# RMSNorm and swish over 16,384 rows: row groups of 32, 36, 28 and 32, rows 48 to 79 loaded in two transfers, rows 32 to 95 stored as 18, 18 and 28

## The chip, the cores and the metric

The kernel runs on one core of one Trainium2 chip. The metric is the device time of one execution in microseconds (us). Before the change the median of three runs is 159.67 us, with the lowest at 159.59 and the highest at 159.82. A difference of under 0.2%, which is 0.32 us here, counts as no change.

## The reference

The input x has 16 x 1024 rows of 512 float32 numbers. Every row is divided by its root mean square, multiplied by gamma, and passed through swish:

```python
rms = np.sqrt(np.mean(x ** 2, axis=-1, keepdims=True) + eps)
x_norm = x / rms * gamma
return (x_norm * (1.0 / (1.0 + np.exp(-x_norm)))).astype(np.float32)
```

So 33.55 MB go in, 33.55 MB come out, and every row is worked on by itself.

## The kernel before

The 16,384 rows are dealt to 128 partitions, so that each partition has 128 rows of 2 KB. From here on "row" means a row of one partition (0 to 127), which stands for 128 rows of x, or 256 KB. The rows are cut into four **groups** (line 28: 32, 48, 16 and 32 rows). A group is a contiguous stretch of x and of the output. Inside it, partition p owns a contiguous run of as many rows as the group has (function `dram`, lines 100 to 106). The group's size is therefore the distance in memory from one partition's piece to the next: 64, 96, 32 and 64 KB. A transfer moves a run of rows for all 128 partitions, and it must lie within one group.

In on-chip memory the rows lie in a **ring** of 96 (line 29). Row a sits at place a modulo 96, and the result is written over the input. Rows 0 to 95 have places of their own. Rows 96 to 127 take the places of rows 0 to 31, so they may be loaded only when the store of rows 0 to 31 has finished.

**Transfers.** All of them are issued by SyncE (SP), in the order of the list `order` (lines 33 to 37), and they all go through one queue. The list holds "load" and "store" entries, "landed" (SP waits until a load has arrived, line 166) and "stored" (SP waits until store 0 has finished, line 169). A store waits itself until enough units have gone through swish (`need` at lines 120 to 123, with the count in `ends`, line 56). Before the change the order is: loads 0, 4, 8, gamma, loads 16, 24, 32, 48, 64, 75; wait until load 64 has landed; store 0 (32 rows, needs four units); load 80; wait until store 0 has finished; loads 96, 112, 125; wait until load 112 has landed; stores 32, 64, 80, 96, 120. A load or store is named here by its first row.

**Compute.** It goes in 16 **units** of 8 rows (`cn`, line 39), numbered from 0. For each unit ScalarE (ACT) squares and sums six of the rows (line 215), VectorE (DVE) the other two (line 251). GpSimd (POOL) makes the factor 1/rms of it (lines 183 and 189). DVE multiplies the unit's rows by the factor and gamma (line 260), and ACT applies swish in one instruction of 4096 elements for each partition (line 225; line 245 for the last two units). ACT's loop squares unit k and then applies swish to unit k - 2. TensorE computes nothing: it passes on that a unit's loads have arrived (lines 172 to 176), so that ACT may start with its squares. Unit k waits for every load that begins in its eight rows.

Of the kernel before, what the change touches and what calls it, by code (L numbers as in the profile page):

```python
# [9 lines left out]
def kernel(  # L10
# [14 lines left out]
    of = out.flatten_outer_dims()  # L25
    R, D = xf.shape

    groups = [32, 48, 16, 32]
    ring = 96
    loads = [(0, 4), (4, 4), (8, 8), (16, 8), (24, 8), (32, 16), (48, 16), (64, 11), (75, 5)]  # L30
    loads += [(80, 16), (96, 16), (112, 13), (125, 3)]
    stores = [(0, 32), (32, 32), (64, 16), (80, 16), (96, 24), (120, 8)]
    order = [("load", a) for a in (0, 4, 8)] + [("gamma", 0)]
    order += [("load", a) for a in (16, 24, 32, 48, 64, 75)]
    order += [("landed", 64), ("store", 0), ("load", 80)]
    order += [("stored", 0), ("load", 96), ("load", 112), ("load", 125)]
    order += [("landed", 112)] + [("store", a) for a in (32, 64, 80, 96, 120)]
    early = 2
    cn = 8
    own = 2  # L40
# [285 lines left out]
```

## Time and profile before

| What | us |
|---|---|
| median of three runs | 159.67 |
| the profiled execution's own time | 159.75 |
| its span, first to last instruction | 158.4 |
| ACT busy | 115.7 (73%) |
| DVE busy | 107.7 (68%) |
| POOL busy | 42.9 (27%) |
| time of the transfers' packets, share of 16 DMA engines' span | 99.1% |

The span begins with the first load's issue. 67.12 MB were moved at a mean of 424 GB/s over it. In the rows for transfers, the time "to landing" counts from the start of the issue on SP to the arrival of the last part. Because the queue works off its transfers one after another, the difference between the landings of two neighbours is the time that the later one took to be moved.

### The profile page before, as it was taken

To read this page: it belongs to the slowest core of one execution; us is meant where nothing else is said; L and a number is where in the kernel's file an instruction comes from. 1 tells how busy PE (TensorE), PEld (TensorE's weight loads), DVE (VectorE), ACT (ScalarE), POOL (GpSimd) and SP (SyncE) were. 2 spreads that over 40 slices of the span, in tenths; PEclk is the share of its full clock that TensorE was granted. 3 is DMA by queue.
4 is the path that set the end of the run, shared out by engine and by line. 5 is a ranking of instruction groups with operands and counts; after the bars stand their busy time and mean duration, and the time that the engine had idled before them with its cause. 6 is when DMAs were issued, how large, how long until landed. Compare 5 with 4: busy or idle time off the path is not lost. (4 is left out here: it accounts for less than half of the span.)

```text
span 158.4 us, 844 instructions
## 1 busy us (share of the span) xinstructions
DVE 107.7 (68%) x198; ACT 115.7 (73%) x205; POOL 42.9 (27%) x38
## 2 busy tenths in 40 slices
DVE  0051899798989889898925989989898995000000
ACT  3608389999999999999459999999999385400000
POOL 1031426060524426060601433516061500000000
DMA  7999999999999979799999999996969999999997
GB/s 257 451 416 443 422 488 439 397 406 497 389 395 565 463 331 530 314 381 480 406 406 472 399 430 400 550 513 281 530 298 488 406 397 455 538 397 397 397 397 331
DMA packets 2744, 67.12 MB, mean 424 GB/s; under 512 B 308, under 2 KB 308, under 8 KB 440
## 3 DMA queue, kind: packets, MB, share of 16 engines
q1 hardware_dynamic: 2744, 67.12, 99.1%
HBM read 33.56 MB, written 33.55 MB: 424 GB/s over the span
## 5 line engine op out<-in xcount | busy, mean ns | idle before, releaser
L260 DVE SCALAR_TENSOR_TENSOR xb<-xb,rstd,gamma_sb 128x512 f32 (+1 forms) x128 | 86.1, 745 | 0.0
L215 ACT ACTIVATE junk<-xb 128x512 f32 (+1 forms) x94 | 54.6, 581 | 13.1 <-ACTq L98 11.3
L225 ACT ACTIVATE xb<-xb x14 | 50.5, 3604 | 0.7 <-ACTq L98 0.7
L251 DVE SCALAR_TENSOR_TENSOR junk_v<-xb 128x512 f32 (+1 forms) x34 | 22.1, 689 | 23.0 <-DVEq L98 23.0
L189 POOL TENSOR_TENSOR rstd<-aeps,neg_half 128x8 f32<-128x8 f32 x16 | 31.7, 1984 | 1.3
L183 POOL TENSOR_SCALAR aeps<-ms 128x8 f32<-128x8 f32 x16 | 10.4, 648 | 79.1 <-DVE junk_v L251 79.1
L215 ACT ACTIVATION_READ_ACCUMULATOR junk<-xb 128x1 f32 x94 | 17.7, 188 | 0.0
L245 ACT ACTIVATE xb<-xb 128x4096 f32<-128x4096 f32 x2 | 7.2, 3616 | 5.0 <-DVE xb L260 5.0
L251 DVE DVE_READ_ACCUMULATOR junk_v<-xb 128x1 f32 x34 | 2.8, 82 | 0.0
L227 ACT ACT_TABLE_LOAD x1 | 1.3, 1283 | 1.9 <-PEq L62 1.9
L269 DVE LOAD_MASK_SELECT gamma_sb<-gamma x1 | 0.0, 14 | 2.0 <-DMA gamma<-in_gamma_dram 2.0
L178 POOL MEMSET gamma<- 128x512 f32 x1 | 0.5, 524 | 1.5 <-POOLq L62 1.5
L269 DVE STREAM_SHUFFLE gamma_sb<-gamma 128x512 f32<-128x512 f32 x1 | 0.7, 719 | 0.0
L307 POOL MEMSET const-float32-0.0<- 128x1 f32 x1 | 0.1, 98 | 0.2 <-issue 0.2
L179 POOL MEMSET neg_half<- 128x8 f32 x1 | 0.1, 104 | 0.0
L307 POOL MEMSET const-bfloat16-1.0<- 128x1 bf16 x1 | 0.1, 103 | 0.0
L307 POOL MEMSET const-uint8-127<- 128x1 uint8 x1 | 0.1, 102 | 0.0
L307 POOL MEMSET const-float32-1.0<- 128x1 f32 x1 | 0.1, 99 | 0.0
## 6 DMA issues: line engine op xcount, KB each, us to landing
xb<-in_x_dram SPq DMA_DIRECT2D x4, 4096.0 KB, 29.9
out_dram<-xb SPq DMA_DIRECT2D x2, 4096.0 KB, 29.8
xb<-in_x_dram SPq DMA_DIRECT2D x3, 2048.0 KB, 14.1
out_dram<-xb SPq DMA_DIRECT2D x1, 6144.0 KB, 22.4
xb<-in_x_dram SPq DMA_DIRECT2D x1, 3328.0 KB, 27.0
xb<-in_x_dram SPq DMA_DIRECT2D x1, 2816.0 KB, 43.1
xb<-in_x_dram SPq DMA_DIRECT2D x2, 1024.0 KB, 6.0
out_dram<-xb SPq DMA_DIRECT2D x1, 2048.0 KB, 21.9
```

Of the source, the lines that this page charges most:

```text
L178: nc.gpsimd.memset(gamma4, 0.0).then_inc(s_zero, 1)
L179: nc.gpsimd.memset(neg_half, -0.5).then_inc(s_half, 1)
L183: nc.gpsimd.tensor_scalar(out=aeps[k % 2], in0=ms[min(k, 1)], scalar1=eps_f, scalar2=None, op0=ALU.add,),
L189: nc.gpsimd.tensor_tensor(out=rstd[:, k * cn : (k + 1) * cn], in0=aeps[k % 2], in1=neg_half, op=ALU.pow),
L215: nc.scalar.activation(out=dummies[j], in_=rows[j], func=AF.Square, scale=inv_d**0.5, accum_out=sums[:, j : j + 1],)
L225: nc.scalar.activation(out=rows, in_=rows, func=AF.Silu).then_inc(s_swish, 1)
L227: nc.scalar.preload_act_table_set("silu_and_others")
L245: nc.scalar.activation(out=rows, in_=rows, func=AF.Silu), s_norm, n + 1
L251: ins = nc.vector.scalar_tensor_tensor(out=junk_v[j], in0=rows[j], scalar=inv_d, in1=rows[j], op0=ALU.mult, op1=ALU.mult, accum_out=to[:, ...
L260: ins = nc.vector.scalar_tensor_tensor(out=rows[j], in0=rows[j], scalar=factors[j], in1=gamma_sb, op0=ALU.mult, op1=ALU.mult,)
L269: need(nc.vector.stream_shuffle(gamma_sb, gamma4, [0] * 32), s_gld, 16).then_inc(s_gamma, 1)
L307: nc = _bacc.Bacc("TRN2", target_bir_lowering=False, num_devices=1)
```

## The change

Three lists and one wait change; no instruction on the compute engines does.

- The groups are 32, 36, 28 and 32 rows for 32, 48, 16 and 32. The distances between the partitions' pieces in the two middle groups become 72 and 56 KB.
- Rows 48 to 79 are loaded as 20 and 12 rows (loads 48 and 68) for 16, 11 and 5 (loads 48, 64 and 75). There is one load fewer.
- Rows 32 to 95 are stored as 18, 18 and 28 rows (stores 32, 50 and 68) for 32, 16 and 16 (stores 32, 64 and 80). The number of stores stays the same.
- Ahead of store 0 SP waits for the landing of load 48, not of load 64.

```diff
-    groups = [32, 48, 16, 32]
+    groups = [32, 36, 28, 32]
     ring = 96
-    loads = [(0, 4), (4, 4), (8, 8), (16, 8), (24, 8), (32, 16), (48, 16), (64, 11), (75, 5)]
+    loads = [(0, 4), (4, 4), (8, 8), (16, 8), (24, 8), (32, 16), (48, 20), (68, 12)]
     loads += [(80, 16), (96, 16), (112, 13), (125, 3)]
-    stores = [(0, 32), (32, 32), (64, 16), (80, 16), (96, 24), (120, 8)]
+    stores = [(0, 32), (32, 18), (50, 18), (68, 28), (96, 24), (120, 8)]
     order = [("load", a) for a in (0, 4, 8)] + [("gamma", 0)]
-    order += [("load", a) for a in (16, 24, 32, 48, 64, 75)]
-    order += [("landed", 64), ("store", 0), ("load", 80)]
+    order += [("load", a) for a in (16, 24, 32, 48, 68)]
+    order += [("landed", 48), ("store", 0), ("load", 80)]
     order += [("stored", 0), ("load", 96), ("load", 112), ("load", 125)]
-    order += [("landed", 112)] + [("store", a) for a in (32, 64, 80, 96, 120)]
+    order += [("landed", 112)] + [("store", a) for a in (32, 50, 68, 96, 120)]
```

## The prediction

> **What bounds the kernel now.** I read the page's busy rows first, then the windows, then the transfers one by one, and last the waits.
>
> The first view is the head of the page, with the row of the DMA queue.
>
> ```profile
> DVE 107.7 (68%) x198; ACT 115.7 (73%) x205; POOL 42.9 (27%) x38
> ...
> DMA  7999999999999979799999999996969999999997
> ...
> q1 hardware_dynamic: 2744, 67.12, 99.1%
> ```
>
> No engine is busy for more than 73%, but the packets fill 99.1% of 16 DMA engines' span. The windows (last two columns: DMA share and GB/s) say the same of the stretch between the ends:
>
> ```profile
> 1.00:158.00 157.00, 107.69 (x198) 115.74 (x205) 42.67 (x34) 1.00 1.00 428
> ```
>
> From 1 us to 158 us the share is 1.00, so there is no room for a gap of more than some 0.5% (the rounding), 0.8 us. (The dips in the 40 slices lie beside slices that are over full; a packet counts where it starts.) So this kernel ends when its bytes have gone through one queue. Only three things can move its end: what a transfer costs beside its bytes, the rate at which bytes move, and the queue running dry.
>
> To get each transfer's time I read its issue on SP and its time to landing. First the timeline of SP, one stretch for each issue (start us, us), then the answers for the transfers issued in the same stretches (KB each, us to landing). In order: loads 24, 32, 48, 64, 75, store 0, load 80; the second fence leaves out the row of store 0, 22.6 us, because it carries no size.
>
> ```profile
> 3.61 0.52 SPq L115 DMA_DIRECT2D xb<-in_x_dram  x1
> 4.17 0.44 SPq L115 DMA_DIRECT2D xb<-in_x_dram  x1
> 4.65 0.44 SPq L115 DMA_DIRECT2D xb<-in_x_dram  x1
> 5.13 0.48 SPq L115 DMA_DIRECT2D xb<-in_x_dram  x1
> 5.66 0.45 SPq L115 DMA_DIRECT2D xb<-in_x_dram  x1
> 48.37 0.35 SPq L121 DMA_DIRECT2D out_dram<-xb  x1
> 48.77 0.43 SPq L115 DMA_DIRECT2D xb<-in_x_dram  x1
> ```
>
> ```profile
> xb<-in_x_dram SPq DMA_DIRECT2D x1, 2048.0 KB, 18.5
> xb<-in_x_dram SPq DMA_DIRECT2D x1, 4096.0 KB, 27.7
> xb<-in_x_dram SPq DMA_DIRECT2D x1, 4096.0 KB, 36.9
> xb<-in_x_dram SPq DMA_DIRECT2D x1, 2816.0 KB, 43.1
> xb<-in_x_dram SPq DMA_DIRECT2D x1, 1280.0 KB, 45.7
> ...
> xb<-in_x_dram SPq DMA_DIRECT2D x1, 4096.0 KB, 32.0
> ```
>
> Start plus time to landing gives when each arrived: load 24 at 22.11, load 32 at 31.87, load 48 at 41.55, load 64 at 48.23, load 75 at 51.36, store 0 at 70.97, load 80 at 80.77. The same sum for the later ones gives 90.50 (load 96), 98.37 (112), 100.26 (125), 119.58 (store 32), 129.27 (64), 139.03 (80), 153.51 (96) and 158.31 (120). The differences are the times to move: 16 rows take 9.76, 9.68, 9.80 and 9.73 as loads, 9.69 and 9.76 as stores; 32 rows take 19.61 (store 0) and 19.32 (store 32). That is about 0.604 us a row, the same for a load, a store, a whole group and a part of one.
>
> Last, the waits of SP up to 60 us, and ACT around store 0's issue.
>
> ```profile
> SPq L166 <- DMA xb<-in_x_dram: 42.1, 1, 42.1
> ```
>
> ```profile
> 44.75 3.60 ACT L225 ACTIVATE xb<-xb  x1
> 48.25 0.58 ACT L215 ACTIVATE junk<-xb 128x512 f32 x1
> ```
>
> Store 0 needs two things: the landing of load 64 (48.23) and the swish of unit 3, which ends at 48.35. They come within 0.12 us of each other, and the store is issued at 48.37. The loads ahead of it in the queue last until 51.36, so the queue does not notice.
>
> **The change, part by part.** All sums are made against the profiled execution, 159.75 us (span 158.4), which is 0.08 above the median of 159.67.
>
> *One load fewer.* Bytes stay the same, so only a transfer's own cost goes. Split stretches of 16 rows take 6.68 + 3.13 = 9.81 (11 and 5) and 7.87 + 1.89 = 9.76 (13 and 3); unsplit loads have a mean of 9.74. That gives 0.02 to 0.07. Small transfers show it better: 5 rows at 0.604 are 3.02, so 0.11 over; 3 rows are 1.81, so 0.08 over. Landings are rounded to 0.1, so the bounds are 0 and 0.13. I take 0.08, nearest to the two small loads: -0.08, on the path, because the queue is never idle. SP also saves an issue of 0.45 us before 6.11 us, which lies beside a wait of 42.1 us and is worth nothing.
>
> *The wait ahead of store 0.* Load 48 now has 20 rows, so it lands at 31.87 + 20 x 0.604 = 43.95. SP then goes on to the store itself, which waits for unit 3's swish, 48.35. The issue moves from 48.37 to 48.38, since the other stores that wait for ACT start 0.03 us after it (109.80 to 109.83). Behind the waiting store stand load 80 and the wait for store 0's end, neither of which may go earlier in any case. Loads 48 and 68 end at 51.28. How late may the store be issued? The first load was issued at 0.00 and landed at 5.0, and its 4 rows move in 2.42, so from issue to first byte it takes at most 2.6 us: bytes from 50.97 at the latest, 0.31 us before the loads are done. So cost nothing; cover 0.31 us by this cautious bound, and every microsecond beyond it is a microsecond at the end.
>
> *Later landings for compute.* Load 48 comes 2.4 us later. Its first user, unit 6, starts squares at 48.25, so 4.3 us remain. Rows 68 to 71 of unit 8 land at 51.28 for 48.23; that unit's squares start at 62.62, 11 us later. ACT has no idle row at all between 30 and 75 us. At no cost: the backlog on ACT hides it. Load 80 and all later loads have the sizes and places in the queue that they had.
>
> *Stores 18, 18 and 28.* Three for three, 64 rows for 64: nothing for the number. They need 7, 9 and 12 units. Seven and nine are ready before the first of them is issued at 98.48; the twelfth unit ends at 109.80, as for the store at row 80 before. The queue is then filled until 100.18 + 36 x 0.604 = 121.9 instead of 129.27, so the cover shrinks from 19 to 12 us and is still cover. Store 96 is issued at 131.11 and the queue is full until 138.95. No cost.
>
> *Distances of 72 and 56 KB between pieces.* No row of this trace has these. The nearest are 64 KB (9.76 and 9.73 for 16 rows loaded), 96 KB (9.68 loaded, 9.69 stored) and 32 KB (9.80 loaded, behind store 0, and 9.76 stored). The extremes are 0.12 apart for 16 rows. Rows 32 to 95 are eight such pieces, in and out together, so the bounds are -1.0 and +1.0 us; as the order by distance has no trend and 0.1 is the rounding, I take 0.
>
> *Sum.* 159.75 - 0.08 + 0 + 0 + 0 + 0 = 159.67 against the profiled execution, and 159.59 on the footing of the median. I forecast 159.6, which is -0.05%: no change that a measurement of this kernel tells apart (0.2%, 0.32 us).
>
> **The rivals.**
>
> *The queue runs dry before store 0 (slower).* The wait for load 64 is replaced by one for unit 3's swish alone. If that swish came later, for instance because unit 5 or 6 waits for load 48's 2.4 us, the store would be issued at 50.8 and its bytes would start at 53.4, 2.1 after the loads: 159.59 + 2.1 = 161.7. It decides once the issue comes later than 48.7; a loss over 0.32 needs 49.0. Against it: unit 3's swish hangs on units up to 5, whose loads end with load 32, which does not change. Chance 0.05.
>
> *The new pieces move more slowly (slower).* At the upper bound it is 159.59 + 1.0 = 160.6, at a third of it 159.9. For it speaks only that no row shows 72 or 56 KB, or load 80 as the tail of a strided group. Chance 0.12, of which 0.09 goes over 0.32.
>
> *The excess of store 0 goes (faster).* Store 0 took 19.61 where store 32 took 19.32. If these 0.29 us are the gap at 51 us or a turn between storing and loading that the new order eases, the time is 159.59 - 0.29 = 159.3; with rounding, 159.2. Against it: store 0 is issued no earlier, and load 80 still follows it. Chance 0.07, of which 0.05 passes the bound.
>
> *A transfer has a large fixed cost (faster).* If each waited for its own completion before the next began, a load fewer would be worth the 2.6 us that bound the first load's start: 157.0. Against it: splits of 16 rows cost at most 0.13. Chance 0.02. The Trainium skill (DMA: Bandwidth & Descriptors, section Anatomy of one DMA — SWDGE (gpsimd) path) gives about 2.0 us fixed for each DMA, which would make 157.6 as an estimate; the landings here disagree, with 3.13 us for a whole transfer of 5 rows behind others.
>
> **How the numbers follow.** The likeliest case has 0.74, and all of it but 0.04 lies within 0.32 us; of those 0.04 I put 0.02 to each side for what 0.14% of spread among the runs does. Faster: 0.05 + 0.02 + 0.02 = 0.09. Slower: 0.05 + 0.09 + 0.02 = 0.16. Same: 0.75. The range runs from 159.2, the third rival's end, to 160.0, which takes in the runs' spread (159.82) and a loss of 0.4 us from the pieces; outside lie the first rival, about half of the second and the fourth, some 0.14.
>
> **What would show it.** Right: the packet count falls by about 144 of 2744, the share from 1 to 158 us stays 1.00, store 0 is issued at 48.3 to 48.4 behind a wait for ACT, load 68 lands near 51.3, load 80 near 80.7, and the last store near 158.2. Wrong: store 0 issued after 49, a share below 1.00 around 51 us, or 18 and 28 stored rows that take more than 10.9 and 16.9 us.

## The result and the profile after

The changed kernel takes 159.98 us (median of 15 runs, 159.80 to 160.41), the kernel before beside it 159.73 us (15 runs, 159.49 to 160.04). The ratio is 1.0019, with a 95% interval of 1.0011 to 1.0028: 0.25 us slower as a difference of medians, inside the 0.32 us that count as no change, but clear of the scatter. The forecast was 159.6 us, a gain of 0.05%.

The head of the page after, busy times and the DMA queue's row:

```profile
DVE 107.7 (68%) x198; ACT 115.7 (73%) x205; POOL 42.8 (27%) x38
...
q1 hardware_dynamic: 2600, 67.12, 98.9%
```

The window from 1 to 158 us of the same kernel (last two columns: DMA share and GB/s):

```profile
1.00:158.00 157.00, 107.67 (x198) 115.74 (x205) 42.65 (x34) 1.00 1.00 428
```

The page shows the same picture as before: the compute engines do the same work, the share from 1 to 158 us is 1.00, and 144 packets are gone. This view books a packet where it starts and takes the mean of the 16 DMA engines, so a short gap on some of them does not show in it. To see where the time went, here are SP's issues of loads 48 and 68, store 0, and loads 80, 96, 112 and 125 after the change (start us, us), and then the answers for the loads among them (KB, us to landing). Store 0, which has no size in its row, landed 23.0 us after its issue.

```profile
4.56 0.44 SPq L115 DMA_DIRECT2D xb<-in_x_dram  x1
5.04 0.48 SPq L115 DMA_DIRECT2D xb<-in_x_dram  x1
48.05 0.35 SPq L121 DMA_DIRECT2D out_dram<-xb  x1
48.44 0.43 SPq L115 DMA_DIRECT2D xb<-in_x_dram  x1
71.03 0.33 SPq L115 DMA_DIRECT2D xb<-in_x_dram  x1
71.40 0.44 SPq L115 DMA_DIRECT2D xb<-in_x_dram  x1
71.88 0.44 SPq L115 DMA_DIRECT2D xb<-in_x_dram  x1
```

```profile
xb<-in_x_dram SPq DMA_DIRECT2D x1, 5120.0 KB, 39.1
xb<-in_x_dram SPq DMA_DIRECT2D x1, 3072.0 KB, 45.9
xb<-in_x_dram SPq DMA_DIRECT2D x1, 4096.0 KB, 32.6
xb<-in_x_dram SPq DMA_DIRECT2D x1, 4096.0 KB, 19.7
xb<-in_x_dram SPq DMA_DIRECT2D x1, 3328.0 KB, 27.5
xb<-in_x_dram SPq DMA_DIRECT2D x1, 768.0 KB, 28.9
```

Start plus time to landing, beside the landings of before:

| Landed | before, us | after, us | after minus before |
|---|---|---|---|
| last load ahead of store 0 (75; 68) | 51.36 | 50.94 | -0.42 |
| store 0 | 70.97 | 71.05 | +0.08 |
| load 80 | 80.77 | 81.04 | +0.27 |
| load 96 | 90.50 | 90.73 | +0.23 |
| load 112 | 98.37 | 98.90 | +0.53 |
| load 125 | 100.26 | 100.78 | +0.52 |
| last store | 158.31 | 158.81 | +0.50 |

The times to landing are rounded to 0.1 us. The trace also has the end of every part of a transfer: each of the 16 DMA engines reports its own share, and the last report is the landing. From here on small differences are taken from these reports. By them the changed kernel comes to store 0 ahead by 0.35 us, of which 0.28 were already there when load 24 landed, and so come from the start. Then store 0 and load 80 together take 30.03 us where they took 29.47. These two transfers have the same rows before and after. Load 112 loses another 0.25 in this execution; behind it the two kernels keep step (by the table 58.03 us from load 125 to the end, before 58.05). I call the place where the 0.56 us are lost **the turn**: the queue goes over from storing to loading, once in the whole execution.

Load 80's parts came within 0.92 us of each other before, and within 1.19 us after. Of the last 64 KB packets of store 0, which normally take 2.42 us, two took over 2.9 us before and six after. A transfer is complete with its slowest engine.

The wide parts show once more, where the queue goes over from loading to storing. SP issues store 32 when the last part of load 112 has landed. The first line is store 32 before the change, the second the run of five stores that begins with store 32 after it:

```profile
98.48 0.34 SPq L121 DMA_DIRECT2D out_dram<-xb  x1
98.95 37.99 SPq L121 DMA_DIRECT2D out_dram<-xb  x5
```

Only load 125, 3 rows, stands in the queue between load 112 and store 32, and the engines that are ahead are through with it before the store's first packets come. Laid out packet by packet, fewer than 12 of the 16 engines have a packet for 0.17 us around 99 us before the change and for 0.70 us after it, with as few as 6 at work in both. After it, ten engines begin store 32 within 0.1 us of each other, which is what engines do that have waited for it. So the queue is not full everywhere, and the change makes this gap wider. In these two executions the gap does not lengthen the run, though: the last engine to begin store 32 does so at 99.87 us before and at 100.39 after, straight after its last packet of load 125, and the last packet of all ends 58.04 us later in both. The slowest engine sets the end, and it was late already.

### The profile page after: what moved, and what is told of

Read it like the earlier page. It is cut to its first block, busy times and chain, and to the rows that moved or that the text cites. A ratio compares the mean times of both kernels' runs of the same rounds, so it can differ in the third digit from the quotient of the medians.

```text
span 158.8 us, 843 instructions
## 1 busy us (share of the span) xinstructions
DVE 107.7 (68%) x198; ACT 115.7 (73%) x205; POOL 42.8 (27%) x38
## 6 DMA issues: line engine op xcount, KB each, us to landing
out_dram<-xb SPq DMA_DIRECT2D x1, 7168.0 KB, 29.4
```

## The experiments

Each ratio is to the kernel before on the same chip, with its 95% interval. "Parts" is how far apart the parts of the named load landed in the profiled execution, and "turn" the time between the landing of the last load ahead of store 0 and that of load 80 there. Both come from one execution each; the ratios are the firmer evidence. The three profiled executions of the changed kernel were among its slower ones (160.17, 160.18 and 160.17 us against medians of 159.98, 159.93 and 159.94). Execution by execution, parts and time go together: over 18 profiled executions, all of the runs below but turn_apart and the changed kernel's first, the parts and that execution's time above the median of before correlate at 0.83. The entries of `order` that follow from a cut of a load or a store are left out of the diffs.

**The two kernels again.** No edit.

> The kernel before once more, as a measure of how far two equal kernels come apart and as a second trace of it. All theories: ratio 1.000, within 0.001. The turn theory (the loss of 0.25 us arises where the queue turns from store 0 to load 80, because load 80 now lies as 32 KB pieces 56 KB apart): store 0 and load 80 together take 29.4 to 29.6 us between landings, as in the first trace of before (29.4).

> The changed kernel once more. All theories but scatter: ratio 1.001 to 1.003. The turn theory: store 0 and load 80 together take 29.9 to 30.1 us between landings again, as in the first trace of after (30.0). The scatter theory (the 0.25 us belong to the draw of the runs): ratio nearer to 1.000 than to 1.002, and the two landings anywhere between.

Measured: before again 1.0000 (0.9990 to 1.0011), turn 29.4 us, parts 0.83. After again 1.0016 (1.0003 to 1.0029), turn 29.9 us, parts 1.36. So the loss is not the draw of the runs, and the turn carries it in a second trace. The twelve times of the changed kernel lie between 159.28 and 160.24: four below 159.5 and eight at 159.85 and over, while ten of before's twelve lie between 159.38 and 159.57. In these runs the loss comes or does not come with an execution, and the change makes it more frequent. The changed kernel's first 15 times and the 11 of its third run below show no such gap, so this is not shown to be general.

**The loads alone, and load 80 in a group of its own.**

```diff
# loads_alone, against the changed kernel
-    groups = [32, 36, 28, 32]
+    groups = [32, 48, 16, 32]
-    stores = [(0, 32), (32, 18), (50, 18), (68, 28), (96, 24), (120, 8)]
+    stores = [(0, 32), (32, 32), (64, 16), (80, 16), (96, 24), (120, 8)]
# own_group_80, against the changed kernel
-    groups = [32, 36, 28, 32]
+    groups = [32, 36, 12, 16, 32]
-    stores = [(0, 32), (32, 18), (50, 18), (68, 28), (96, 24), (120, 8)]
+    stores = [(0, 32), (32, 18), (50, 18), (68, 12), (80, 16), (96, 24), (120, 8)]
```

> Groups and stores as before, only the loads of 20 and 12 rows and the wait for load 48. Turn theory (geometry of load 80): no loss, 0.08 us saved, ratio 0.9995 and store 0 with load 80 at 29.4 us. Loads theory (20 and 12 rows, or the earlier wait, put the queue's engines out of step): ratio 1.0015 to 1.002, and the 30.0 us at the turn are there. Stores theory (18, 18 and 28 rows move more slowly): ratio 0.9995, since the stores are the old ones.

> The changed kernel, but rows 68 to 79 and 80 to 95 in groups of their own, so that load 80 is one contiguous stretch as before; the store of 28 rows becomes 12 and 16, one store more (0.08 us). Turn theory: ratio 1.000 to 1.0005 and store 0 with load 80 at 29.4 us. Loads theory: ratio 1.0015 to 1.0025, 30.0 us. Stores theory (18 rows): about half of the loss or more stays, ratio 1.001 to 1.002, turn at 29.4 us.

Measured: loads_alone 1.0034 (1.0021 to 1.0047, six runs), turn 30.1 us, parts 1.47. own_group_80 1.0009 (0.9996 to 1.0023), turn 29.1 us, parts 0.59. My first theory, that the new geometry of load 80 makes the turn dear, falls: with the old groups and stores and an unchanged load 80 the loss is all there. New group sizes and stores of 18 and 28 rows are not needed for it. What is left of the change is the loads of 20 and 12 rows and the earlier wait. The second run does not tell the theories apart: its turn was good in the profiled execution (159.49 us, one of its faster ones), and its interval takes in both 1.000 and 1.002.

**Which part of the loads.**

```diff
# wait_48_alone, against before
-    order += [("landed", 64), ("store", 0), ("load", 80)]
+    order += [("landed", 48), ("store", 0), ("load", 80)]
# no_small_load, against before; the wait for load 48 as well
-    loads = [..., (48, 16), (64, 11), (75, 5)]
+    loads = [..., (48, 16), (64, 16)]
# loads_20_7_5, against loads_alone; the wait is for load 68
-    loads = [..., (48, 20), (68, 12)]
+    loads = [..., (48, 20), (68, 7), (75, 5)]
```

> The kernel before with the wait for load 48 in place of load 64, and nothing else. Theory of the wait: the changed wait is what makes the turn from store 0 to load 80 dear; ratio 1.002 to 1.004, and load 80's 16 parts land 1.2 to 1.5 us apart. Theory of the pieces (the sizes of the loads ahead of store 0 decide): ratio 1.000, the parts 0.6 to 0.9 us apart, since in the kernels already run store 0 is issued at 48.0 to 48.1 us under either wait.

> The kernel before with rows 64 to 79 as one load of 16 rows, and the wait for load 48: one transfer fewer, no load of 20 or 12 rows, no small load right ahead of store 0. Theory of the small load (without a small last load the 16 DMA engines enter store 0 out of step, and the turn costs more): ratio 1.002 to 1.004, load 80's parts 1.2 to 1.5 us apart. Theory of the 20 rows: ratio 0.9995, parts 0.6 to 0.9 us apart, 0.08 us saved.

> Groups and stores as before; rows 48 to 79 as 20, 7 and 5 rows with the wait for the load of 7. It is the earlier run with 20 and 12 rows, but with the small load ahead of store 0 again. Theory of the small load: ratio 1.000, load 80's parts 0.6 to 0.9 us apart. Theory of the 20 rows: ratio 1.002 to 1.004, parts 1.2 to 1.5 us apart.

Measured: the wait alone 0.9995 (0.9984 to 1.0005), parts 0.48; no loss shows. 20, 7 and 5 rows 0.9996 (0.9981 to 1.0011), parts 0.41: with a small load behind it the load of 20 rows costs nothing either. Without the small load 1.0004 (0.9994 to 1.0014), parts 1.15: the profile shows the wide parts, but the time doesn't show a loss clear of zero, and the 1.002 to 1.004 that this theory expected were missed. So far the theory of the small load stands, weakly in the one run that should have been slow.

**The turn taken apart.**

```diff
# turn_apart, against the changed kernel
-    order += [("landed", 48), ("store", 0), ("load", 80)]
-    order += [("stored", 0), ("load", 96), ("load", 112), ("load", 125)]
+    order += [("landed", 48), ("store", 0), ("stored", 0), ("load", 80)]
+    order += [("load", 96), ("load", 112), ("load", 125)]
```

> The changed kernel, but load 80 waits until store 0 has finished, so that store 0's end and load 80's head cannot overlap; the queue stands empty for a round trip in between. Turn theory: load 80's parts land within 0.7 us of each other, the queue's packets show no slow ones around 67 to 71 us, the times of the runs lie within 0.3 us of each other where the changed kernel's lay 1.0 apart, and the time is 160.9 to 162.0 (the best runs of the changed kernel, 159.3, with a gap of 1.6 to 2.6 us). If the loss lies elsewhere (stores of 18 and 28 rows, loads 96 to 125): the runs stay 0.7 us or more apart.

Measured: 161.85 us (161.78 to 162.14, five runs), 1.0125 (1.0106 to 1.0143). The runs lie 0.36 us apart, a little over the 0.3 expected. The issue of load 68, store 0 and load 80 in this kernel, and the answers for load 68 and load 80; store 0's answer was 22.2 us.

```profile
5.03 0.44 SPq L115 DMA_DIRECT2D xb<-in_x_dram  x1
...
48.45 0.35 SPq L121 DMA_DIRECT2D out_dram<-xb  x1
...
70.70 0.33 SPq L115 DMA_DIRECT2D xb<-in_x_dram  x1
```

```profile
xb<-in_x_dram SPq DMA_DIRECT2D x1, 3072.0 KB, 46.3
...
xb<-in_x_dram SPq DMA_DIRECT2D x1, 4096.0 KB, 12.4
```

Load 68 lands at 51.33 and store 0 at 70.65: 19.32 us, as store 32 took before the change with no load behind it, and not the 19.61 of before or the 20.11 of after. One such number is weak evidence, since a landing is that of the slowest engine: in the traces with 32 rows in store 32 it took 19.32 to 19.36 us where load 125's parts lay 0.8 us or more apart and 19.54 to 19.69 where they lay closer. At the mean of the 16 parts it is clearer. Store 0 takes 19.33 us here and 19.74 to 19.98 in all 18 other traces in which its 32 rows are one transfer. None of its last 16 packets took more than 2.48 us. So the slow packets at the end of store 0 come with load 80's reads behind it; that much is shown. It is not yet the loss, because this mean is 19.74 to 19.82 with eight loads ahead of store 0 and 19.75 to 19.98 with nine: what differs is how unevenly the engines come out of the turn. Parts of load 80: 0.76, a little over the 0.7 expected, and in this execution the parts of load 68, ahead of the turn, lay 0.86 apart already. The empty queue costs more than it saves: load 80 takes 12.45 us from store 0's landing, 2.7 over the 9.74 of a load behind others.

**Small load or number of loads.** In the trace of every kernel so far, the ones with nine loads ahead of store 0 had narrow parts, and most of those with eight wide ones. A small load ahead of store 0 and a ninth load were the same thing until here. These runs part them.

```diff
# after_small, against the changed kernel
-    loads = [..., (48, 20), (68, 12)]
+    loads = [..., (48, 20), (68, 7), (75, 5)]
# after_split_early, against the changed kernel
-    loads = [..., (32, 16), (48, 20), (68, 12)]
+    loads = [..., (32, 11), (43, 5), (48, 20), (68, 12)]
```

> The changed kernel with its load of 12 rows cut into 7 and 5, so that a small load stands ahead of store 0 again; groups, stores and the wait are the changed ones. Theory of the small load: ratio to before 0.999 to 1.001, at least 0.2 us below the changed kernel on the same chip, load 80's parts at most 0.95 us apart. Theory that the new groups or stores carry the loss: ratio 1.0015 to 1.003 as for the changed kernel.

> The changed kernel with load 32 cut into 11 and 5 rows: as many transfers ahead of store 0 as before the change, but the small one 20 us earlier, and 12 rows right ahead of store 0. Theory of the small load ahead of store 0: no help, ratio 1.0015 to 1.003, load 80's parts 1.1 to 1.5 us apart. Theory of the count (the number of transfers ahead, whatever their sizes, decides): ratio 0.999 to 1.001, parts at most 0.95 us apart.

> The changed kernel on the chip of the two runs with split loads, for comparison. All theories: ratio 1.001 to 1.003 and load 80's parts 1.1 to 1.5 us apart; if the ratio is 1.000 here, the loss depends on the chip.

> Old groups and stores with the loads of 20 and 12 rows, once more. Theory of the small load: ratio 1.002 to 1.004 as in its first run, parts 1.1 to 1.5 us apart. If the first ratio of 1.0034 came from the few runs (six), it is nearer to 1.001.

Measured on one chip: after_small 1.0006 (0.9997 to 1.0015), parts 0.82; after_split_early 0.9997 (0.9989 to 1.0006), turn 29.6 us, parts 1.01; the changed kernel for the third time 1.0009 (1.0000 to 1.0018), turn 30.2 us, parts 1.52; loads_alone again 1.0020 (1.0009 to 1.0030), turn 30.0 us, parts 1.29. The theory of the small load falls too: the run with the cut 20 us earlier, and 12 rows right ahead of store 0, is as fast as before. The count of nine is what it shares with after_small. After_small is a weaker case: its median is 0.16 us below the changed kernel's on this chip (159.78 and 159.94), where at least 0.2 was expected, and the two ratios' intervals overlap for the most part. Of the other expectations, a parts limit of 0.95 was missed slightly by 1.01, and the changed kernel's 1.0009 lies just under the 1.001 expected.

**More loads, and other sizes at the turn.**

```diff
# after_10, against the changed kernel: both cuts
+    loads = [..., (32, 11), (43, 5), (48, 20), (68, 7), (75, 5)]
# before_10, against before
-    loads = [..., (48, 16), ...]
+    loads = [..., (48, 11), (59, 5), ...]
# head_small, against the changed kernel
-    loads += [(80, 16), ...]
+    loads += [(80, 3), (83, 13), ...]
# tail_small, against the changed kernel
-    stores = [(0, 32), ...]
+    stores = [(0, 28), (28, 4), ...]
```

> The changed kernel with both cuts, load 32 as 11 and 5 and load 68 as 7 and 5: ten loads ahead of store 0. Theory of the count (more transfers ahead, less loss): ratio 0.999 to 1.0005, load 80's parts at most 0.95 us apart. Theory of the place (only some places in the queue are good, nine transfers being one): ratio 1.001 to 1.003 is as likely, with parts over 1.1 us apart.

> The kernel before with load 48 cut into 11 and 5: ten loads ahead of store 0. Theory of the count: ratio 0.999 to 1.0005 (one transfer more costs 0.08 us), parts at most 0.95 us apart. Theory of the place: ratio 1.001 to 1.003, parts over 1.1 us, together with the other run of ten loads.

> The changed kernel with load 80 cut into 3 and 13 rows: eight loads ahead of store 0, small packets (6 KB) at the head of what follows it. Count or place of what is ahead: still slow, ratio 1.001 to 1.003, load 83's parts over 1.1 us apart. Theory of the sizes at the turn (small reads disturb the store's tail less): ratio 0.999 to 1.0005, parts at most 0.95 us.

> The changed kernel with store 0 cut into 28 and 4 rows, so that the last packets of the store have 8 KB in place of 64. Theory of the sizes at the turn: the delay of the slowest engine falls, parts of load 80 at most 0.8 us apart, ratio 0.998 to 1.000. Theory of the count of loads ahead of store 0: eight are eight, ratio 1.001 to 1.003. Theory of the count of all transfers ahead of load 80 (ten as before the change): ratio 0.999 to 1.0005.

Measured: ten loads, 1.0009 (1.0000 to 1.0018) with parts of 0.62, and 1.0008 (0.9999 to 1.0017) with parts of 0.73. The turn stays good with ten, as the theory of the count has it, but the time is 0.13 us above before's nine loads, more than the 0.08 expected for a transfer. Both ratios lie between the range of the count's theory and that of the place's, and their intervals reach into both, so here the parts alone speak for the count. head_small 1.0011 (1.0002 to 1.0020), load 83's parts 1.47; tail_small 1.0016 (1.0006 to 1.0026), parts 1.05 (it also waits for both pieces of the store ahead of load 96). Small packets on either side of the turn did not help, though each of these two kernels also has one transfer more. With tail_small ten transfers stand ahead of load 80, as before the change: so in this run the count of all transfers did not help.

**Two stores fewer.**

```diff
# fewer_stores, against before
-    groups = [32, 48, 16, 32]
+    groups = [32, 64, 32]
-    stores = [(0, 32), (32, 32), (64, 16), (80, 16), (96, 24), (120, 8)]
+    stores = [(0, 32), (32, 32), (64, 32), (96, 32)]
-    order += [("landed", 112)] + [("store", a) for a in (32, 64, 80, 96, 120)]
+    order += [("landed", 112)] + [("store", a) for a in (32, 64, 96)]
# fewer_stores_20_7_5: also
-    loads = [..., (48, 16), (64, 11), (75, 5)]
+    loads = [..., (48, 20), (68, 7), (75, 5)]
-    order += [("landed", 64), ("store", 0), ("load", 80)]
+    order += [("landed", 68), ("store", 0), ("load", 80)]
```

> The kernel before with groups of 32, 64 and 32 and stores of 32, 32, 32 and 32 rows: two stores fewer, loads as before, nine ahead of store 0. If a transfer costs 0.08 us by itself: ratio 0.999 (0.16 us less). If the 0.13 us of the tenth load are the transfer itself: 0.9983. If it costs nothing: 1.000. All with load 80's parts at most 0.95 us apart, as the count of loads ahead is unchanged. The last store waits for unit 15's swish (136.4 us) and the queue is full to 138.9 us, so a cover of 2.5 us; if that is too little, ratio over 1.000.

> The same, with rows 48 to 79 loaded as 20, 7 and 5 rows and the wait for the load of 7. Nine loads ahead of store 0. By the theory that their number decides: the same ratio as the run above within 0.001. If sizes decide and 20, 7 and 5 is the better cut: 0.0005 to 0.001 below it, with parts at most 0.6 us apart.

Measured: 0.9988 (0.9979 to 0.9997), and 0.9986 (0.9977 to 0.9995), with parts of 0.60 and 0.72. Both are faster than the kernel before, just clear of the scatter and inside the 0.32 us that count as no change; the changed kernel did not run beside them. With two stores fewer and nine loads ahead of store 0 kept, the first gains 0.12% of 159.93, which is 0.19 us, or 0.10 us for each store (0.02 to 0.17 by the interval). The edit also puts rows 32 to 95 in one group, with 128 KB between pieces, so the gain is not shown to be the stores' alone. The profiles do not show where it lies: from the last engine's start on store 32 to the last packet these two take 58.43 us, and five kernels with as narrow parts and more stores 58.35 to 58.52. The last store of fewer_stores:

```profile
136.12 0.33 SPq L121 DMA_DIRECT2D out_dram<-xb  x1
```

It is issued when unit 15 is through. The store ahead of it lands at 139.14, 3.0 us later, and the last store's 32 rows then take 19.32 us, so the larger last store does not leave the queue dry.

All kernels but turn_apart in the order of the loads ahead of store 0:

| Loads ahead | kernel | ratio | parts, us |
|---|---|---|---|
| 8 | after: first, again, third | 1.0019, 1.0016, 1.0009 | 1.19, 1.36, 1.52 |
| 8 | loads_alone: first, again | 1.0034, 1.0020 | 1.47, 1.29 |
| 8 | no_small_load, own_group_80 | 1.0004, 1.0009 | 1.15, 0.59 |
| 8 | head_small, tail_small | 1.0011, 1.0016 | 1.47, 1.05 |
| 9 | before (first profile), before again | 1, 1.0000 | 0.92, 0.83 |
| 9 | wait_48_alone, loads_20_7_5 | 0.9995, 0.9996 | 0.48, 0.41 |
| 9 | after_small, after_split_early | 1.0006, 0.9997 | 0.82, 1.01 |
| 9, two stores fewer | fewer_stores, with 20, 7 and 5 rows | 0.9988, 0.9986 | 0.60, 0.72 |
| 10 | after_10, before_10 | 1.0009, 1.0008 | 0.62, 0.73 |

own_group_80, head_small and tail_small have one transfer more than the changed kernel.

## Why the prediction was wrong

*What bounds the kernel* held in the main: the share from 1 to 158 us is 1.00 in both, and compute hides. The packets fell by 144 as said, and store 0 was issued at 48.05 behind ACT:

```profile
SPq L121 <- ACT xb L225: 4.3, 1, 4.3
```

Load 68 landed at 50.94, where 51.3 was said, but load 80 at 81.04 for 80.7 and the last store at 158.81 for 158.2. That "the queue is never idle" holds for the slowest engine only; others have the gap at 99 us.

*One load fewer, -0.08 us.* The size was right. From the landing of load 24 to that of the last load ahead of store 0, at the mean of the 16 parts, the 48 rows take 29.14 to 29.19 us in all ten traces with eight loads, 29.22 or 29.23 in all eight with nine, and 29.29 or 29.30 with ten: 0.07 us for each load. But the step looked at the transfer's own cost alone. Along with the load something else changed: the turn took 29.80 to 30.24 us in six traces with eight loads ahead of store 0 (29.09 in own_group_80; head_small, tail_small and turn_apart, which alter the turn itself, left out), and 29.17 to 29.63 with nine. Over the nine comparisons with eight loads the mean ratio is 1.0015 (1.0017 without the three that have one transfer more), over the four edited kernels with nine and all their stores 0.9999; the difference of 1.0015 and 0.9999 is 0.26 us, the size of the loss.

*"Load 80 and all later loads have the sizes and places in the queue that they had."* This is the step that failed: with this sentence the turn from store 0 to load 80 got no term in the sum. Load 80 had the same rows and stood behind the same store, and yet store 0 and load 80 together went from 29.47 to 30.03 us. The prediction took the duration of a transfer from a row as a property of the transfer. At the turn it goes with what ran ahead, 20 us earlier.

*The wait ahead of store 0, at no cost:* right, wait_48_alone gives 0.9995 (0.9984 to 1.0005). *Stores of 18, 18 and 28 rows, at no cost:* right; they took 10.88, 10.89 and 16.92 us, where 10.9 and 16.9 were said, the slowest engine's way from store 32 to the end is 58.04 us in both kernels, and after_split_early, which has these stores, 0.9997. *Distances of 72 and 56 KB, at no cost:* right by the same run, with 0.9989 to 1.0006; the bounds of 1.0 us either way were far too wide.

*The rivals.* None was the one that came. The third saw the right place: it named store 0's excess of 0.29 us over store 32 and a turn between storing and loading, and turn_apart bears out that such an excess belongs to the turn. But I gave the place only one sign, a gain if the excess went, and asked nowhere what would make it larger. The row for that was at hand: a store that takes 19.61 with a load behind it and 19.32 without one has a price that is not fixed by its bytes, so it can move both ways. The measured 159.98 lies just inside the range of 159.2 to 160.0, but its upper end was made from the runs' spread and from a loss by the new pieces, which did not come. That the range holds the time is luck.

**What stays open:** why nine loads ahead of store 0 make the turn milder than eight. Sizes of the loads, where the cut lies, the wait, the packets on either side of the turn and the count of all transfers ahead of load 80 have been tried, most of them in one run each, and none of them accounts for it. Nor does how far out of step the engines come to store 0: the parts of the last load ahead of it lie 0.37 to 0.78 us apart with eight loads (turn_apart left out) and 0.34 to 0.63 with nine. Seven loads were not tried. The count itself is a regularity over these kernels, with own_group_80's parts as an exception and no_small_load's time as a weak case, and not a mechanism.

## What to carry to other kernels

When one queue is nearly full from end to end, a load less was worth 0.07 us in the stretch where it stood, and more than that was lost where the queue goes over from storing to loading: the change with its merged loads lost 0.19% in all, and the edit that merged stores gained 0.12%. Where a row for the same bytes has two durations in one trace, as 19.61 and 19.32 us here, find out what stands beside the dearer one before counting any of it as fixed. A loss that came with some executions and not others showed here in how far apart the 16 engines landed, so look at the scatter of the times beside their median, and at which execution was profiled.

## What the hardware showed that was not expected

Store 0's last packets are slowed when the reads of load 80 are queued behind it: 64 KB packets of 2.42 us took up to 3.47 us in the changed kernel and up to 3.61 us in loads_alone, and at most 2.48 us when the load was held back. Holding it back costs 2.7 us of empty queue, so the overlap is still the better bargain.

Not all of a good turn comes back at the end. With 20, 7 and 5 rows the last load landed 0.54 us earlier than in before's first profile (99.74 against 100.28 by the last part's report), and the last packet ended only 0.13 us earlier (157.78 against 157.91). Where load 125's parts lie wide apart, the engines fall in step at the gap at 99 us, because those ahead wait there for store 32: in the changed kernel the parts lie 1.44 us apart at load 125 and 0.51 at store 32, and the engines' last packets end within 0.31 us of each other. From the last engine's start on store 32 such executions take 58.04 us to the last packet, eleven of them to the hundredth. Where the parts are narrow there is little or no gap and no falling in step: with 20, 7 and 5 rows they lie 0.42 us apart at load 125 and 0.79 at store 32, one engine ends 0.48 us after the other fifteen, and the stretch takes 58.52 us. Why that engine falls behind is open.

The engines that waited did not speed up the others. In the changed kernel the 6 KB packets of load 125 took 0.24 us at the mean while 15 or 16 engines were at work and 0.23 us while 10 or fewer were.
